# A gated linear attention and short convolution layer on one core: v and z_a with the rows of h as TensorE weights, block turns on VectorE, and two heads per attention step

## The chip, the core and the metric

The kernel runs on one core of a Trainium2 chip. The metric is device time in microseconds (us) for one execution; less is better. The engines are TensorE (PE, matmuls; PEld is its weight load), VectorE (DVE), ScalarE (ACT), GpSimd (POOL) and SyncE (SP, which issues the DMAs here). Each executes its own instructions strictly in order and waits on semaphores for the others.

## The reference

One layer (DEPTH = 1) on a sequence of 1024 rows of width 1024, all in float32:

```python
h = rms_norm(x, norm_mix_g)
q, k, v, z_a, gk_low, cb, cc, xc, z_c, g_a, g_c = split(h @ w_in)   # 512, 512, 1024, 1024, 16, 6 x 1024
gk = log_sigmoid(gk_low @ w_gk2 + b_gk) / 16
o = gla_chunked(q, k, v, gk)        # 4 heads, key width 128, value width 256, chunks of 64
o = rms_norm(o per head, gla_norm_g)
y_a = (o * silu(z_a)) @ w_branch_a
u = causal_dwconv3(cc * xc)
y_c = (cb * u * silu(z_c)) @ w_branch_c
merged = sigmoid(g_a + b_ga) * y_a + sigmoid(g_c + b_gc) * y_c
x = x + merged @ w_out
x = x + sigmoid(rms_norm(x, norm_ple_g) @ w_ple_gate) * (p @ w_ple_proj)
out = rms_norm(x, norm_final_g)
```

In `gla_chunked`, b is the running sum of gk within a chunk; q is scaled with exp(b), k with exp(-b) for the scores and with exp(b_last - b) for the state. The output is the masked scores times v plus scaled q times the state; the state decays by exp(b_last) per chunk and adds k^T v.

## The kernel before

**Numbers and products.** Float32 matmuls are done in three passes over a high and a low part (`split` at line 580 makes hi by a ScalarE copy and lo by a VectorE subtract; `mm3` at line 591 issues the three matmuls). The large products use a seven-product scheme of the Strassen kind on 2 x 2 blocks: h's seven combinations `hres[0..6]` (hi and lo, 512 x 512 each) stay in SBUF, and a `Cell` (line 704) computes 256 columns of a projection. It loads four weight blocks, `ring_steps` (line 663) makes the seven weight combinations, each split, and `product` runs twelve 512-column matmuls. In a cell the 128 columns of a weight combination are TensorE's stationary operand and the h rows (time) are the moving one, so the result has the projection's columns on partitions and time along the free axis. Each cell uses three PSUM banks: X, Y and V (tags m0 to m5, two sets in turn). Two more banks have the tag "o", two buffers, for everything else.

**Order.** Every instruction is first noted (`note`, line 260) and at the end put in order by a planner in the kernel (`put_in_order`, line 406), which has costs of its own and keeps the main matmuls in program order while it places the side ones among them; buffers of a tag are handed out in program order. `emit` (line 484) issues all of them, so the profile shows line 491 everywhere and one goes by names. Side work is given as generators: `weave` starts one, each `tick` (two per product) advances it, and `yield n` makes it wait for n ticks. DMAs are all issued on SyncE's queue.

**Stages.** (1) Start to 76 us: nine warm matmuls on zeros, p W_pe (`pe_blocks`, line 974), the norm of x in two halves (`scale_h`, line 943: squares, `ms` matmuls with ones, root on POOL and VectorE, `rt` transposes, scaling), two products of each of the eight gate cells (`two_products`, line 997; names ga0p to gc3p), and h's combinations. (2) 76 to 170 us: four v cells. `v_cons` (line 1037) copies each result block if needed, turns it with four 128 x 128 transposes on TensorE (matmuls against an identity, `pt_v`), splits it and stores it to DRAM (vd). `decays` (line 1059) runs woven beside them: for each half of the sequence `lowp` (16 matmuls), a copy `low`, four `zp` matmuls, one per head; for each pair of heads Abs, Exp and Ln on ScalarE, subtracts and scans on VectorE, and stores to DRAM (cd). It yields 2 after each zp and 4 after each pair. (3) 170 to 246 us: q and k cells, which read cd and store the scaled operands (qkd). (4) 246 to 322 us: four z_a cells; `za_cons` (line 1182) makes silu(z_a) times the norm's gain and stores it (szd). (5) 322 to 627 us: sixteen convolution cells, with w_out and w_ple_gate prepared beside them (wtd). (6) 627 to 780 us: gate cells, and woven among them attention (`attend`, line 1271), one head and 128 rows per step, with operands in four rotating buffers. A step transposes the keys on TensorE (X from ident and qkl), forms the scores, the state's growth and the output, and three steps later transposes the normed output (op from ident and og), multiplies it with silu(z_a) and stores it (od). (7) 780 to 935 us: y_c, then y_a with the merge. (8) From 935 us: the output projection, `flip` (line 1511), which transposes the new x on TensorE (`pt_g`) for the last gate, and that gate with the final norm.

Of the kernel before, what the change touches and what calls it, by code (L numbers as in the profile page):

```python
# [9 lines left out]
F32 = mybir.dt.float32  # L10
# [39 lines left out]
class View:  # L50


    def __init__(self, buf, rows, off, dims, dtype):
        self.buf, self.rows, self.off, self.dims, self.dtype = buf, rows, off, dims, dtype

# [75 lines left out]

    def place(self):
        real = self.buf.get()
        if self.dtype != self.buf.dtype:
# [368 lines left out]
def kernel(  # L503
# [4 lines left out]
    wb: bass.AP,  # L508
    wgl: bass.AP,
# [54 lines left out]
    qkd = [[dram(f"qkd{h}_{i}", NP, 5 * P) for i in range(2)] for h in range(H)]  # L564
    vd = [[dram(f"vd{h}_{i}", NP, 2, DV) for i in range(2)] for h in range(H)]
    szd = [[dram(f"szd{h}_{i}", NP, 2, P) for i in range(2)] for h in range(H)]
# [96 lines left out]
    def ring_steps(name, side, raw, fresh):  # L663
# [3 lines left out]
        def put(src):  # L667
            hi = bp.tile([P, 4, P], F32R, tag="whi", name=f"{name}hi", bufs=RING)
            lo = bp.tile([P, 4, P], F32R, tag="wlo", name=f"{name}lo", bufs=RING)
            split(hi, lo, src)  # L670
            return hi, lo
# [32 lines left out]
    class Cell:  # L704


        def __init__(self, name, side, src, res, cons, prods=ORDER, begin=None, s1=None, u2=None, s5=None, fresh=()):
# [5 lines left out]
            self.steps, self.fresh = ring_steps(name, side, self.raw, fresh), fresh  # L713
# [132 lines left out]


    def gate_cons(c, bias, dst):
        def cons(i, j, src):
            k = 2 * c + j  # L850
            t = ev(f"g{k}_{i}")
            act(t, src, AF.Sigmoid, bias=bias[:, k:k + 1])
            store(dst[k][i], t)
        return cons
# [12 lines left out]
    def merge_a(c, pool):  # L867
        def cons(i, j, src):
# [5 lines left out]
            tt(g, src, g, op=ALU.mult)  # L874
            if i == 0 and k >= 4:
                t = late[k - 4] = bp.tile([P, 512], F32, tag="raw", name=f"m{k}", bufs=8)
                tt(t, g, m, op=ALU.add)
                g = t
            else:
                tt(g, g, m, op=ALU.add)  # L880
            store(md[i][:, :, k // 4, :, k % 4, :], g.rearrange("p (a b t) -> p a b t", a=2, b=2))
# [5 lines left out]
    for n, name in enumerate([f"v{h}" for h in range(4)] + ["q0", "k0", "q1", "k1"] + [f"za{h}" for h in range(4)]  # L887
                             + [f"{m}{g}" for g in range(4) for m in ("cc", "xc", "zc", "cb")]
# [144 lines left out]

    with phase("v", [ph["prep0"]]) as qp:
        def v_cons(h):
            def cons(i, j, src):
                if j == 1:
                    t = src
                else:
                    t = ev(f"vt{h}_{i}_{j}")  # L1040
                    nc.scalar.copy(t, src)

                def flip():
                    pt = pso.tile([P, 4, P], F32, tag="o", name=f"pt_v{h}_{i}_{j}", bufs=2)
                    for s in range(4):
                        transpose(pt[:, s, :], t[:, s * P:(s + 1) * P])
                    hi = qp.tile([P, 4, P], F32R, tag="vhi", name=f"vhi{h}_{i}_{j}", bufs=2)
                    lo = qp.tile([P, 4, P], F32R, tag="vlo", name=f"vlo{h}_{i}_{j}", bufs=2)
                    split(hi, lo, pt)
                    js = slice(j * P, (j + 1) * P)  # L1050
                    store(vd[h][i][:, :, 0, js], f(hi))
                    store(vd[h][i][:, :, 1, js], f(lo))
                    return
                    yield

                weave(flip(), 2)
            return cons

        def decays():
# [14 lines left out]
            g2raw = qp.tile([P, 512], F32, name="g2raw")  # L1074
# [4 lines left out]
            yield 2  # L1079
            for half in range(2):  # L1080
# [14 lines left out]
                yield 2  # L1095
                for hp in range(2):
                    t1 = qp.tile([P, 2, HALF], F32, tag="t1", name=f"t1_{half}{hp}")
                    c = qp.tile([P, 2, HALF], F32, tag="c4", name=f"c4_{half}{hp}")
                    for i in range(2):
# [5 lines left out]
                        nc.vector.tensor_scalar(c[:, i, :], zp, bgk[:, h:h + 1], 0.0, op0=ALU.add, op1=ALU.min)  # L1105
                        yield 2
                    act(t1, t1, AF.Exp, scale=-1.0)
                    act(t1, t1, AF.Ln, bias=1.0)
                    for i in range(2):
                        tt(t1[:, i, :], t1[:, i, :], c[:, i, :], op=ALU.subtract)  # L1110
                        nc.vector.tensor_tensor_scan(c[:, i, :], smask, t1[:, i, :], 0.0, op0=ALU.mult, op1=ALU.add)
                        store(cd[2 * hp + i][half], c[:, i, :])
                    yield 4

        vs = [Cell(f"v{h}", "B", W[f"v{h}"], hres, v_cons(h)) for h in range(4)]
        vs[0].begin = lambda: weave(decays(), 1)
# [4 lines left out]
        run_groups(single(vs), single(qks[:2]))  # L1121
        finish_woven()

    with phase("qk", [ph["v"]]) as qp:
# [7 lines left out]
        def q_cons(hp):  # L1132


            def cons(i, j, src):
# [19 lines left out]
                store(qkd[h][i][:, :, 0:P], f(hi))  # L1155
                store(qkd[h][i][:, :, P:2 * P], f(lo))
                store(qkd[h][i][:, :, 2 * P:3 * P], Qf[:, :, P:2 * P])
            return cons

        def k_cons(hp):  # L1160

            def cons(i, j, src):
# [13 lines left out]
                store(qkd[h][i][:, :, 3 * P:5 * P], kk.rearrange("p n s t -> p n (s t)"))  # L1176
# [5 lines left out]
        def za_cons(h):  # L1182
            def cons(i, j, src):
                t = ev(f"sz{h}_{i}_{j}")
                act(t, src, AF.Sigmoid)
                stt(t, src, ggla[:, j:j + 1], t, op0=ALU.mult, op1=ALU.mult)
                store(szd[h][i][:, :, j, :], t.rearrange("p (n t) -> p n t", t=P))
            return cons

        zas = [Cell(f"za{h}", "B", W[f"za{h}"], hres, za_cons(h)) for h in range(4)]  # L1190
        run_groups(single(qks), single(zas[:2]))


    with phase("conv", [ph["qk"]]) as vp:
        def weights(vp):


            for w in range(2):
                for kt in range(4):
                    t = vp.tile([P, 4, 512], F32, tag="wt", name=f"wt{w}_{kt}", bufs=2)  # L1200
                    load(t, wb[w][:, :, kt, :].rearrange("n p c -> p n c"))
                    yield 14
                    b11, b12, b22, b21 = (t[:, n] for n in range(4))
                    if w:
                        for n, q in enumerate((b11, b12, b22, b21)):
                            k = kt + 4 * (n >= 2)
                            act(q, q, AF.Copy, scale=gple[:, k:k + 1])
                            if n != 1:
                                store(wtd[w][4 + (n + 1) // 2][:, kt, :], q)
                    tt(b11, b12, b11, op=ALU.subtract)  # L1210
                    yield 2
                    tt(b12, b22, b12, op=ALU.subtract)
                    yield 2
                    tt(b22, b22, b11, op=ALU.subtract)
                    yield 2
                    tt(b21, b21, b22, op=ALU.subtract)
                    for n, q in enumerate((b11, b22, b12, b21)):
                        store(wtd[w][n][:, kt, :], q)
                    yield 4

# [40 lines left out]

        gas, gcs = ([Cell(f"{m}{c}", "B", W[f"{m}{c}"], hres, gate_cons(c, bias, dst), prods=(1, 2, 4, 5, 6),
                          s1=s1d[n + c]) for c in range(4)]
                    for n, m, bias, dst in ((0, "ga", bga, gad), (4, "gc", bgc, gcd)))
        weave(weights(vp), 20)
        run_groups(single(zas + convs), pairs(gas[:2]))
        finish_woven()

    def attend(hp, ap, every):

        its = [(pr, 2 * hp + i) for pr in range(2 * NP) for i in range(2)]
        n, LAG = len(its), 3
        ins, szs, ogs, scores, S, Sp = {}, {}, {}, {}, {}, {}
        for i in range(2):
            h = 2 * hp + i
            S[h] = ap.tile([P, DV], F32, tag=f"S{i}", name=f"S{h}")  # L1280
            Sp[h] = (ap.tile([P, DV], F32R, tag=f"Sh{i}", name=f"Sh{h}"),
                     ap.tile([P, DV], F32R, tag=f"Sl{i}", name=f"Sl{h}"))

        def fetch(it):
            pr, h = its[it]
            nm = f"{h}_{pr}"
            qk = ap.tile([P, 5 * P], F32R, tag="qkl", name=f"qkl{nm}", bufs=4)
            v = ap.tile([P, 2, DV], F32R, tag="vl", name=f"vl{nm}", bufs=4)
            load(f(qk), qkd[h][pr // NP][:, pr % NP])
            load(f(v), vd[h][pr // NP][:, pr % NP])  # L1290
            ins[it] = qk, v

        def step_a(it, X):
            pr, h = its[it]
            qk = f(ins[it][0])
            mm(X[:, 0:P], qk[:, 3 * P:4 * P], qk[:, 2 * P:3 * P], start=True, stop=True)
            if pr < 2 * NP - 1:
# [401 lines left out]
```

## Time and profile before

| | |
|---|---|
| time, median of 3 runs | 1109.24 us (1108.81 to 1109.28) |
| span of the profiled execution | 1107.6 us (the page gives this span; what lies around it is not recorded) |
| TensorE busy | 1096.7 us (99%), 5113 records |
| VectorE busy | 857.5 us (77%), 1381 records |
| ScalarE busy | 592.5 us (53%), 1106 records |
| DMA moved | 235.81 MB, mean 213 GB/s |

The span is first to last instruction of one execution. Matmuls overlap in the pipeline, so the mean duration of one is longer than the distance between two starts. Rows of groups, the timeline and the chain of waits give, in this order, the engine, the operation, the tile written and those read (buffer numbers left out), the tile's shape and a count.

### The profile page before, as it was taken

What the parts mean: (1) busy time and instruction counts of PE and PEld (TensorE: products, weight loads), DVE (VectorE), ACT (ScalarE), POOL (GpSimd) and SP (SyncE); (2) the same over time, 40 slices, a digit from 0 to 9 for tenths busy, and PEclk for the clock granted to TensorE, in tenths of its full rate; (3) what the DMA queues carried; (4) which work ended last, traced back from release to release, by engine and by line L of the source; (5) the groups of instructions that cost most, each with busy time, mean ns of one, the idle gap of its engine ahead of it and who ended that gap; (6) DMA issues with size and microseconds to landing.
All of it is one profiled execution on the core that took longest, in us unless ns stands there. A gap on an engine that the chain in (4) does not pass through costs nothing.

```text
span 1107.6 us, 15420 instructions
## 1 busy us (share of the span) xinstructions
PE 1096.7 (99%) x5113; PEld 914.5 (83%) x5113; DVE 857.5 (77%) x1381; ACT 592.5 (53%) x1106; POOL 55.9 (5%) x121
## 2 busy tenths in 40 slices
PE   9999999999999999999999999999999999999996
PEld 7888888888888888888888888898888888888885
DVE  6997786997876856757648687876999879868666
ACT  6766765555464433333343376765836445457554
POOL 0000000000000000000000022230000000002012
PEclk9999999999999999999999999999999999999999
DMA  9943467988995131221312599998595888889753
GB/s 319 320 165 100 147 197 240 276 246 274 326 354 177 48 103 49 67 87 48 99 54 67 184 306 348 311 290 301 182 329 181 294 266 279 295 309 302 257 201 114
DMA packets 159040, 235.81 MB, mean 213 GB/s; under 512 B 12785, under 2 KB 74481, under 8 KB 155889
## 3 DMA queue, kind: packets, MB, share of 16 engines
q1 hardware_dynamic: 158960, 234.83, 64.0%
q8 instruction: 40, 0.66, 0.2%
q14 instruction: 40, 0.32, 0.1%
HBM read 154.04 MB, written 80.74 MB: 212 GB/s over the span
## 4 chain that ended last, share of the span: by engine, by line
PE 98%; DVE 1%; ACT 0%; DMA 0%; POOL 0%; issue 0%; POOLq 0%; DVEq 0%; ACTq 0%
PE op L491 3%; PE pe L491 2%; PE X L491 2%; PE ga3Y L491 1%; PE ga2Y L491 1%; PE ga1Y L491 1%; PE ga0Y L491 1%; PE out1Y L491 1%; PE gc1Y L491 1%; PE gc0Y L491 1%; PE out0Y L491 1%; PE out3Y L491 1%; PE v2Y L491 1%; PE v1Y L491 1%; PE out2Y L491 1%; PE v3Y L491 1%
## 5 line engine op out<-in xcount | busy, mean ns | idle before, releaser
L491 ACT ACTIVATE junk<-x 128x512 bf16<-128x512 f32 (+1 forms) x29 | 17.9, 616 | 13.6 <-DVE x L491 12.8
L491 POOL MEMSET t<- 128x2 f32 x8 | 0.8, 100 | 443.8 <-DVE u L491 270.9
L491 DVE TENSOR_TENSOR wt<-wt 128x512 f32<-128x512 f32 x32 | 21.6, 686 | 0.5 <-DMA zc0raw<-in_wc_dram 0.3
L491 POOL TENSOR_TENSOR or<-or,mhalf 128x1 f32<-128x1 f32 x32 | 20.4, 639 | 2.7
L491 DVE SCALAR_TENSOR_TENSOR u<-t,vec,u 128x1024 f32<-128x1024 f32 x16 | 20.4, 1277 | 0.0
L491 ACT ACTIVATE og<-op,or 128x256 f32<-128x256 f32 x32 | 15.1, 472 | 8.8 <-POOL or L491 6.5
L491 DVE COPY_PREDICATED aT<-trim,X 128x128 f32<-128x128 int32 x32 | 9.6, 301 | 12.8 <-PE X L491 12.4
L491 POOL TENSOR_SCALAR rg<-ms 128x1 f32<-128x1 f32 x8 | 4.8, 602 | 266.0 <-ACT junk L491 265.9
L491 ACT ACT_TABLE_LOAD x12 | 15.4, 1283 | 0.9 <-PEq L1688 0.7
L491 ACT CAST aTh<-aT 128x128 fp32r<-128x128 f32 x32 | 9.5, 298 | 11.2 <-DVE aT L491 9.7
L491 PE MATMUL op<-vl,aTh 128*128 128x256 f32 x64 | 15.0, 314 | 0.0
L491 POOL TENSOR_SCALAR or<-oms 128x1 f32<-128x1 f32 x32 | 8.8, 275 | 119.0 <-ACT junk L491 119.0
L491 PE MATMUL op<-Sh,qkl 128*128 128x256 f32 x56 | 14.6, 283 | 0.0
L491 DVE TENSOR_TENSOR oT<-op,szl 128x256 f32<-128x256 f32 x32 | 13.4, 420 | 1.0 <-DMA od<-oT 0.6
L491 ACT ACTIVATE junk<-op 128x256 bf16<-128x256 f32 x32 | 12.3, 385 | 2.0 <-PE op L491 1.6
L491 PE MATMUL pe<-wpehi,pThi 128*128 128x512 f32 x32 | 13.1, 409 | 0.0
L491 DVE TENSOR_TENSOR Sl<-S,Sh 128x256 fp32r<-128x256 f32 x28 | 11.8, 420 | 1.4 <-ACT Sh L491 1.3
L491 DVE TENSOR_TENSOR vlo<-pt_v,vhi 128x512 fp32r<-128x512 f32 x16 | 10.6, 681 | 2.8 <-ACT vhi L491 2.8
L491 PE MATMUL pe<-wpelo,pThi 128*128 128x512 f32 x32 | 12.8, 400 | 0.0
L491 PE MATMUL pe<-wpehi,pTlo 128*128 128x512 f32 x32 | 12.7, 398 | 0.0
L491 PEld LDWEIGHTS X<-vl,keh 128*128 128x128 f32 x56 | 10.5, 188 | 2.3
L491 PE MATMUL X<-qkl 128*128 128x128 f32 x64 | 12.3, 273 | 0.0
(3245 smaller groups left out, 4183.6 us busy)
## 6 DMA issues: line engine op xcount, KB each, us to landing
wtd<-wt SPq DMA_DIRECT2D x44, 256.0 KB, 4.0
qkl<-qkd SPq DMA_DIRECT2D x32, 320.0 KB, 5.1
wt<-in_wb_dram SPq DMA_DIRECT2D x8, 1024.0 KB, 7.0
vl<-vd SPq DMA_DIRECT2D x32, 256.0 KB, 5.1
wgq<-wtd SPq DMA_DIRECT2D x7, 1024.0 KB, 8.3
uq<-ud SPq DMA_DIRECT2D x5, 1024.0 KB, 5.5
oq<-od SPq DMA_DIRECT2D x5, 1024.0 KB, 6.7
hq<-in_xT_dram SPq DMA_DIRECT2D x8, 512.0 KB, 6.9
```

What stands on the lines that cost most here:

```text
L491: o.call(*[place(a) for a in o.args], **{k: place(a) for k, a in o.kw.items()})
```

## The change

- **v and z_a** are no longer cells. A new function `wide` computes all 1024 columns of each with h's rows as the stationary operand and the weights as the moving one (512 columns), so the results have time on partitions. Four row blocks are in work at once: eight PSUM banks, the fourth of each set of four with tag "o". The seven products run in the order 0, 3, 1, 2, 5, 4, 6. z_a follows v directly; q and k come after it. The blocks need no transpose: v is split and stored, z_a becomes z times sigmoid(z).
- **decays** yields 1 everywhere; its c tile is now one buffer per head with two buffers in all.
- **k**'s state operand is turned in blocks of 32 x 32 on VectorE and put in place by the DMA's addresses (ked). So are attention's output and the operand of the last gate; the columns of the a-gates, w_ple_gate and its norm gain are permuted to match.
- **attention** takes two heads per step, reads its operands through two rotating buffers in the slots of hres 0 and 3, multiplies the output with silu(z_a) ahead of the turn, and yields 3 per step. The norm's gain is applied later, as twenty ScalarE scalings of 128 x 512 when y_a's operands are read.

The diff, cut to its core:

```diff
+    def put_blocks(dst, start, dims, src):
+        store(dst.spread(start, dims), src)
...
+    def wide(name, w, pool, cons):
+        raw, ring, keep = {}, {}, {}
...
+        def product(k, acc, start):
+            rhi, rlo = hres[k]
+            for kt in range(4):
+                whi, wlo = ring.pop((k, kt))
+                for b in range(4):
+                    bs = slice(b * P, b * P + P)
+                    nc.side = False
+                    mm3(acc[b], rhi[:, kt, bs], rlo[:, kt, bs], whi, wlo, start and kt == 0, kt == 3)
+                    nc.side = True
+                    if b % 2:
+                        tick()
...
+        first, second = ("m0", "m1", "m2", "o"), ("m3", "m4", "m5", "o")
+        near = [(bp, "u2"), (bp, "u2"), (bp, "s5"), (bp, "s5")]
+        prep(0)
+        X = four("X", first)
+        prep(3)
+        product(0, X, True)
+        x0 = copies("x", X, near)
+        prep(1)
+        product(3, X, False)
+        for b in range(4):
+            cons(0, 0, b, X[b])
+        prep(2)
+        V = four("V", second)
+        product(1, V, True)
+        Y = four("Y", first)
+        for b in range(4):
+            nc.scalar.copy(Y[b], x0[b])
+        c22 = copies("s", V, [(bp, "s5"), (bp, "s5"), (pool, "ws"), (pool, "ws")])
...
-                def flip():
-                    pt = pso.tile([P, 4, P], F32, tag="o", name=f"pt_v{h}_{i}_{j}", bufs=2)
-                    for s in range(4):
-                        transpose(pt[:, s, :], t[:, s * P:(s + 1) * P])
...
+        def v_cons(i, j, b, src):
+            hi = qp.tile([P, 512], F32R, tag="vhi", name=f"vhi{i}_{j}_{b}", bufs=2)
+            lo = qp.tile([P, 512], F32R, tag="vlo", name=f"vlo{i}_{j}_{b}", bufs=2)
+            split(hi, lo, src)
+            for n, t in enumerate((hi, lo)):
+                store(vd[j][i][:, b, :, n, :], f(t).rearrange("p (h d) -> p h d", h=2))
...
-                    c = qp.tile([P, 2, HALF], F32, tag="c4", name=f"c4_{half}{hp}")
+                    c = [qp.tile([P, HALF], F32, tag="c4", name=f"c4_{half}{hp}{i}", bufs=2) for i in range(2)]
...
-                        yield 2
+                        yield 1
...
-                    yield 4
+                    yield 1
...
-        vs[0].begin = lambda: weave(decays(), 1)
+        weave(decays(), 1)
+        wide("v", [wv[0, n] for n in range(4)], qp, v_cons)
+        finish_woven()
+        wide("za", [wv[1, n] for n in range(4)], qp, z_cons)
...
+                nc.vector.transpose(turned.rearrange("p b n c -> p n b c"),
+                                    kf[:, :, P:2 * P].rearrange("p n (b c) -> p n b c", c=32))
+                for g in range(4):
+                    put_blocks(ked[hp][i][:, j, g * P:g * P + P], j * 512 + g * P, [(32 * 1024, 4), (1, P)],
+                               turned[32 * g:32 * g + 32].rearrange("p b n c -> p b (n c)"))
...
+        vb, qb = slot(0, "h", f"v{hp}", (2, 1024)), slot(0, "l", f"qk{hp}", (2, 1024))
...
+            for h in range(2):
+                stt(sz[:, h], op[:, h], r[:, h:h + 1], sz[:, h], op0=ALU.mult, op1=ALU.mult)
...
+            nc.vector.transpose(turns[i][:, :, m, :], sz.rearrange("p h (b c) -> p (h b) c", c=32))
...
+            if s and s + 1 < n:
+                fetch(s + 1)
+            yield 3
...
+            if gain is not None:
+                for kt in range(4):
+                    act(t[:, kt, :], t[:, kt, :], AF.Copy, scale=gain[:, kt % 2:kt % 2 + 1])
...
-                pt = pso.tile([P, 4, P], F32, tag="o", name=f"pt_g{p}_{i}_{j}", bufs=2)
-                for k in range(4):
-                    transpose(pt[:, k, :], xt[i][j][:, k * P:(k + 1) * P])
-                g = lp.tile([P, 4, P], F32, tag="gr", name=f"gr{p}_{i}_{j}", bufs=3)
-                nc.scalar.copy(g, pt)
-                store(gd[p][j][:, i], g)
+                g = lp.tile([P, 16, 32], F32, tag="gr", name=f"gr{p}_{i}_{j}", bufs=3)
+                nc.vector.transpose(g, xt[i][j].rearrange("p (b c) -> p b c", c=32))
+                for a in range(4):
+                    put_blocks(gd[p][j][:, i, a, :], i * 512 + a * P, [(32 * 1024, 4), (1, P)],
+                               g[32 * a:32 * a + 32].rearrange("p (b k) c -> p b (k c)", k=4))
```

More of the change, by code (lines that the diff above doesn't have):

```diff
@@ L130, in blocks, with spread @@
         return sorted({b for s in starts for b in range(s // GRAIN, (s + step * (n - 1)) // GRAIN + 1)})
+    def spread(self, start, dims):
+        v = View(self.buf, self.rows, self.off, self.dims, self.dtype)
+        v.apart = start, dims
+        return v
     def place(self):
         real = self.buf.get()
+        if self.apart:
+            start, dims = self.apart
+            return bass.AP(tensor=real.tensor, offset=real.offset + start,
+                           ap=[[self.buf.size, 32]] + [[s, n] for s, n in dims])
         if self.dtype != self.buf.dtype:
@@ L508 @@
     wb: bass.AP,
+    wv: bass.AP,
     wgl: bass.AP,
@@ L1032, with need, put, prep @@
     nc.vector.tensor_scalar(ggla, ggla, float(P) ** -0.5, None, op0=ALU.mult)
-    with phase("v", [ph["prep0"]]) as qp:
[L1035 to L1041, printed above, removed]
-                def flip():
-                    pt = pso.tile([P, 4, P], F32, tag="o", name=f"pt_v{h}_{i}_{j}", bufs=2)
-                    for s in range(4):
-                        transpose(pt[:, s, :], t[:, s * P:(s + 1) * P])
[L1047 to L1057, printed above, removed]
+    def wide(name, w, pool, cons):
+        raw, ring, keep = {}, {}, {}
+        def need(n, kt):
+            raw[n, kt] = bp.tile([P, 512], F32, tag="raw", name=f"{name}raw{n}_{kt}", bufs=8)
+            load(raw[n, kt], w[n][:, kt, :])
+        def put(k, kt, src):
+            hi = bp.tile([P, 512], F32R, tag="whi", name=f"{name}{k}hi{kt}", bufs=RING)
+            lo = bp.tile([P, 512], F32R, tag="wlo", name=f"{name}{k}lo{kt}", bufs=RING)
+            split(hi, lo, src)
+            ring[k, kt] = hi, lo
+        B11, B12, B22, B21 = range(4)
+        def prep(k):
+            for kt in range(4):
+                if k in (0, 3, 6):
+                    need(B11 if k == 0 else B21, kt)
+                elif k in (1, 2):
+                    need(B12 if k == 1 else B22, kt)
+                at = lambda n: raw[n, kt]
+                if k == 1:
+                    keep[kt] = bp.tile([P, 512], F32, tag="T", name=f"{name}T{kt}", bufs=4)
+                    tt(keep[kt], at(B12), at(B11), op=ALU.subtract)
+                elif k == 2:
+                    tt(keep[kt], at(B22), keep[kt], op=ALU.subtract)
+                elif k == 4:
+                    tt(at(B12), at(B22), at(B12), op=ALU.subtract)
+                elif k == 6:
+                    tt(keep[kt], at(B21), keep[kt], op=ALU.subtract)
+                put(k, kt, keep[kt] if k in (1, 2, 6) else at({0: B11, 3: B21, 4: B12, 5: B22}[k]))
+        def product(k, acc, start):
[9 more added lines that the diff above has]
+                        tick()
+        def four(what, tags):
+            return [psm.tile([P, 512], F32, tag=t, name=f"{name}{what}{b}", bufs=2 if t == "o" else 1) for b, t in enumerate(tags)]
+        def copies(what, acc, tags):
+            out = []
+            for b in range(4):
+                where, tag = tags[b]
+                t = where.tile([P, 512], F32, tag=tag, name=f"{name}{what}{b}", bufs=2)
+                nc.scalar.copy(t, acc[b])
+                out.append(t)
+            return out
+        first, second = ("m0", "m1", "m2", "o"), ("m3", "m4", "m5", "o")
[13 more added lines that the diff above has]
+        Y = four("Y", first)
+        for b in range(4):
+            nc.scalar.copy(Y[b], x0[b])
+        c22 = copies("s", V, [(bp, "s5"), (bp, "s5"), (pool, "ws"), (pool, "ws")])
+        prep(5)
+        product(2, Y, False)
+        c12 = copies("u", Y, [(bp, "u2"), (bp, "u2"), (pool, "wu"), (pool, "wu")])
+        prep(4)
+        product(5, V, False)
+        for b in range(4):
+            tt(c12[b], V[b], c12[b], op=ALU.add)
+            cons(0, 1, b, c12[b])
+        prep(6)
+        product(4, Y, False)
+        for b in range(4):
+            tt(c22[b], Y[b], c22[b], op=ALU.add)
+            cons(1, 1, b, c22[b])
+        product(6, Y, False)
+        for b in range(4):
+            cons(1, 0, b, Y[b])
@@ L1073, in decays @@
                 split(glw[:, 8:12, i, 0:16], glw[:, 8:12, i, 16:32], gdif)
-            g2raw = qp.tile([P, 512], F32, name="g2raw")
+            g2raw = qp.tile([P, 512], F32, tag="low", name="g2raw")
             load(g2raw, wgk2)
@@ L1180 @@
             qks[2 * hp].cons, qks[2 * hp + 1].cons = q_cons(hp), k_cons(hp)
[L1182 to L1219, printed above, removed]
+        vp = phase("conv", [ph["qk"]])
         convs = []
@@ L1260, with weights @@
                 convs.append(Cell(f"{m}{g}", "B", W[f"{m}{g}"], hres, cons, begin=cc_begin if m == "cc" else None))
+        run_groups(single(qks), single(convs[:2]))
+    with vp:
+        def weights(vp):
+            for w in range(2):
+                for kt in range(4):
+                    t = vp.tile([P, 4, 512], F32, tag="wt", name=f"wt{w}_{kt}", bufs=2)
+                    load(t, wb[w][:, :, kt, :].rearrange("n p c -> p n c"))
+                    yield 14
+                    b11, b12, b22, b21 = (t[:, n] for n in range(4))
+                    if w:
+                        for n, q in enumerate((b11, b12, b22, b21)):
+                            k = kt + 4 * (n >= 2)
+                            act(q, q, AF.Copy, scale=gple[:, k:k + 1])
+                            if n != 1:
+                                store(wtd[w][4 + (n + 1) // 2][:, kt, :], q)
+                    tt(b11, b12, b11, op=ALU.subtract)
+                    yield 2
+                    tt(b12, b22, b12, op=ALU.subtract)
+                    yield 2
+                    tt(b22, b22, b11, op=ALU.subtract)
+                    yield 2
+                    tt(b21, b21, b22, op=ALU.subtract)
+                    for n, q in enumerate((b11, b22, b12, b21)):
+                        store(wtd[w][n][:, kt, :], q)
+                    yield 4
         gas, gcs = ([Cell(f"{m}{c}", "B", W[f"{m}{c}"], hres, gate_cons(c, bias, dst), prods=(1, 2, 4, 5, 6),
@@ L1397 @@
     with phase("att", [ph["conv"]]) as ap:
-        aTf = [ap.tile([P, P], F32, name=f"aT{i}") for i in range(2)]
+        aTf = [ap.tile([P, 2, P], F32, name=f"aT{i}") for i in range(2)]
         for a in aTf:
@@ L1645, in _lay_out @@
     col = lambda m, n: m[:, n * 256:n * 256 + 256]
-    cells = [col(v, h) for h in range(4)]
+    cells = []
     for hp in range(2):
         cells += [col(q, hp), col(k, hp)]
-    cells += [col(za, h) for h in range(4)]
     for g in range(4):
```

270 lines of the change are left out of this document (132 added, 138 removed).

## The prediction

> **What bounds the kernel now.** I read the page first: busy times, granted clock and the chain that ended last.
>
> ```profile
> span 1107.6 us, 15420 instructions
> PE 1096.7 (99%) x5113; PEld 914.5 (83%) x5113; DVE 857.5 (77%) x1381; ACT 592.5 (53%) x1106; POOL 55.9 (5%) x121
> PEclk9999999999999999999999999999999999999999
> PE 98%; DVE 1%; ACT 0%; DMA 0%; POOL 0%; issue 0%; POOLq 0%; DVEq 0%; ACTq 0%
> ```
>
> TensorE (PE) is busy 1096.7 of 1107.6 us, at full clock in every slice, and holds 98% of the chain. A share over the whole span can hide a stage with slack, so I next took the windows by stage (columns: stretch, its length, then busy time and instructions of PE, PEld, VectorE (DVE), ScalarE (ACT) and POOL, the clock, the DMA share and GB/s).
>
> ```profile
> 30.00:76.00 46.00, 46.00 (x215) 38.35 (x213) 43.51 (x57) 33.47 (x48) 1.02 (x1) 1.00 0.75 260
> 76.00:170.00 94.00, 93.99 (x442) 76.70 (x441) 76.67 (x119) 63.01 (x101) 0.64 (x2) 1.00 0.51 154
> 170.00:246.00 76.00, 76.00 (x339) 62.93 (x338) 63.36 (x127) 42.23 (x88) 0.00 (x0) 1.00 0.84 254
> 627.00:780.00 153.00, 153.00 (x877) 134.02 (x875) 114.60 (x266) 99.69 (x269) 29.24 (x64) 1.00 0.91 301
> 780.00:860.00 80.00, 80.00 (x354) 66.27 (x353) 78.17 (x103) 47.02 (x68) 0.00 (x0) 1.00 0.71 238
> ```
>
> These are the end of the gate preparation, the v cells with the decays, the q and k cells, attention, and the stage after it. PE has no hole in any of them. So PE work that goes is gained in full, and every wait the new order puts before a matmul is lost in full. VectorE is the next bound: 43.51 of 46, and 78.17 of 80 after attention.
>
> **What goes.** The transposes on PE, 220 in all, are these groups (last columns: busy us, mean ns, idle before).
>
> ```profile
> L491 PE MATMUL op<-ident,og 128*128 128x128 f32 x64 | 12.3, 273 | 0.0
> L491 PE MATMUL X<-ident,qkl 128*128 128x128 f32 x28 | 7.6, 273 | 0.0
> L491 PE MATMUL pt_g<-ident,x 128*128 128x128 f32 x48 | 7.4, 272 | 0.0
> L491 PE MATMUL pt_v<-ident,vt 128*128 128x128 f32 x32 | 5.0, 273 | 0.0
> L491 PE MATMUL pt_g<-ident,x2r 128*128 128x128 f32 x16 | 2.4, 272 | 0.0
> ```
>
> The other 32 for v carry names of partial sums (v0s and the like). The 273 ns is no price, because matmuls overlap; what counts is the distance from start to start, in the timeline:
>
> ```profile
> 102.22 0.28 PE L491 MATMUL pt_v<-ident,vt 128*128 128x128 f32 x1
> 102.33 0.64 PE L491 MATMUL pt_v<-ident,v0s 128*128 128x128 f32 x4
> 102.81 0.49 PE L491 MATMUL pt_v<-ident,vt 128*128 128x128 f32 x3
> 103.06 0.47 PE L491 MATMUL v1V<-h1hi,v1hi 128*128 128x512 f32 x1
> 103.37 0.39 PE L491 MATMUL v1V<-h1lo,v1hi 128*128 128x512 f32 x1
> ```
>
> Eight transposes take 103.06 - 102.22 = 0.84 us (0.105 each), or 0.115 each if the late start of the second v1V matmul is theirs. So 220 x 0.11 = **24.2 us less PE work** (23.1 to 25.3). All other matmuls stay in number and size, v and za included; only weights and moving operand change places. Their price, with a cold one beside it, is in the chain of waits:
>
> ```profile
> 1.44 4.21 PE warm L491 x9
> 76.39 2.72 PE v0X L491 x12
> 92.49 3.73 PE lowp L491 x16
> ```
>
> A 512-column matmul takes 2.72/12 = 0.227 us; the first nine of the kernel, just after idleness, 4.21/9 = 0.468.
>
> **What is added, hidden or not.** VectorE gets 40 block turns of 512 elements, for which no row stands. The nearest are 0.69 (128x512 subtract, below) and 1.22 (scan, below); I take the first, since a turn has no carry from element to element: 28 us, of which merging two heads into one instruction in attention gives part back. VectorE has 857.5 of 1107.6, so this is hidden if it falls evenly: 8 turns in the q and k stage (5.5 to 9.8 us against 12.6 idle there), 16 in attention (38 idle), 16 at the output. ScalarE loses the transposes' evictions and gets 20 scalings of attention's output (about 0.6 each by the copy row below, 12 us in a stage where it is half idle). SyncE's queue gets 28 more DMAs, many with runs of 512 bytes. I put 1.0 us for what of all this is not covered (0 to 10).
>
> **Start, 0 to 76 us.** The planner reorders it, as the instruction order shows. Before:
>
> ```profile
> 16.99 1.23 DVE L491 TENSOR_TENSOR sq<-sq 128x1024 f32<-128x1024 f32 x1 [0.37 <-ACT sq L491]
> 19.40 1.68 PE ms L491 x16
> 21.08 2.44 PE pe L491 x10
> 71.93 1.21 DVE L491 TENSOR_TENSOR hq<-hq,hq 128x1024 f32<-128x1024 f32 x1
> 73.06 1.21 DVE L491 TENSOR_TENSOR h4lo<-hq,h4hi 128x1024 fp32r<-128x1024 f32 x1
> ```
>
> The sum of squares is ready at 18.22, and the ms matmuls come after 57 pe matmuls. Now they come after 48: 9 x 0.24 = 2.2 us earlier, at 17.2, so PE waits 1.0. The root behind ms (POOL, then VectorE) was covered by ten matmuls (2.44); three are left (0.7), so PE waits up to 1.7, which I take whole: the rows show that ten matmuls cover it, not with how much to spare. Later, four more splits of h (pitch 73.06 - 71.93 = 1.13, 4.5 us) stand ahead of the split that the second gate product needs, in a stretch where VectorE is 95% busy; earlier v splits no longer stand there, which gives back most: 1.8 (0 to 4.5). **Start: +4.5** (1.0 to 7.2).
>
> **The v stage.** Four row blocks now share two sets of PSUM banks. The fourth bank of each set carries the tag "o" with two buffers, handed out in program order: X3, lowp, four zp, lowp, four zp, V3, Y3. The decays yield every tick, so all of them are noted within the first two products, and PE executes in order. What was beside PE work before now stands before matmuls. Durations, from the timeline of before and the tile views of cd (the last line but one) and vd (the last):
>
> ```profile
> 131.47 0.58 ACT L491 COPY v2s<-v2V 128x512 f32<-128x512 f32 x1
> 131.95 0.69 ACT L491 ACTIVATE t<-zp,vec 128x512 f32<-128x512 f32 x1
> 132.65 1.28 ACT L491 ACT_TABLE_LOAD   x1
> 132.67 0.75 DVE L491 TENSOR_SCALAR c<-zp,vec 128x512 f32<-128x512 f32 x1 [0.18 <-ACT t L491]
> 133.95 1.06 ACT L491 ACTIVATE t<-t 128x1024 f32<-128x1024 f32 x1
> 136.02 1.28 ACT L491 ACT_TABLE_LOAD   x1
> 137.31 1.06 ACT L491 ACTIVATE t<-t 128x1024 f32<-128x1024 f32 x1
> 138.41 0.69 DVE L491 TENSOR_TENSOR t<-t,c 128x512 f32<-128x512 f32 x1 [2.17 <-ACT t L491]
> 140.22 1.22 DVE L491 TENSOR_TENSOR_SCAN c<-smask,t 128x512 f32<-128x512 f32 x1
> DMA to landing us min/median/max: 2.1/3.7/5.1
> DMA to landing us min/median/max: 2.6/4.2/6.8
> ```
>
> Table load and function are 2.34 us together. Step by step, by the order of instructions:
> - Product 3 may write X1 to X3 only after ScalarE has copied them out; the copies stand between two table pairs: 4 x 0.58 + 2 x 2.34 = 7.0 us against 19 matmuls (4.3). Part of an Abs (0.69) lies ahead of it: **3.05** (2.7 to 3.4).
> - Second half's zp0 waits for low's copy, which stands behind Abs, both table pairs and two copies: 3 x 0.58 + 2 x 2.34 + two or three VectorE pieces (1.4 to 2.1) = 7.8 to 8.5, against lowp (3.73) and 8 matmuls (1.82): **2.45**.
> - zp1 needs X3's bank, freed by the fourth vlo, behind two scans and two splits on VectorE: 2 x 1.22 + 3 x 0.69 = 4.5, less zp0's own 0.2 and 0.08 for each piece, the difference of pitch and duration above: **3.9** (3.5 to 4.3); zp2 waits 0.5 for zp0's eviction.
> - V3 needs the bank of zp2. Its eviction (c of the second pair) needs c's buffer, which the first pair's scan result leaves only once stored to cd. From zp1: Abs 0.69, two table pairs 4.68, two subtracts 1.3, scan 1.2, landing 2.1 to 5.1, eviction 0.75 = 10.7 to 13.7, less 0.7 of matmuls: 10.0 to 13.0. I take **10.5**, nearer the short end, since the DMA share is only 0.51 here. Behind V3 stand all remaining matmuls of v.
>
> Sum 20.4 (18.9 to 24.2). **At za's first product**, X1 and X2 wait for the last v splits: vhi and vlo have two buffers each, and a third split waits until the first is stored. A cast (as the 0.58 copy), landing 2.6 to 4.2, cast and split of the third block (1.3) and a weight's split between (0.69) make 5.1 to 6.7, against 15 matmuls (3.4): 1.7 to 3.3. Two blocks wait in turn, so I go near the long end: **3.2**.
>
> **Cold clock.** No row of before shows PE after an idle of 10 us except the kernel's start: nine matmuls at 0.468 instead of 0.227 lose 2.2 us. I take that once, after V3's wait (0 to 4.4).
>
> The Trainium skill, "TensorE: Matmul & The Clock Gate", section "Why this matters for your kernels", warns of PE idle gaps above about 3 us, after which the clock falls to half. By it the clock would fall once or more here; the start row agrees with it, while no gap of before can test it.
>
> **Sum**, against the profiled span: 1107.6 - 24.2 + 4.5 + 20.4 + 3.2 + 2.2 + 1.0 = 1114.7. The time median (1109.24) lies 1.6 above that span, which I keep: **1116.3 us**, 0.6% slower. With all ends one way: 1107.6 - 25.3 + 1.0 + 18.9 + 1.7 = 1103.9 (1105.5 as time), and the other way 1107.6 - 23.1 + 7.2 + 24.2 + 3.3 + 4.4 + 10 = 1133.6 (1135.2).
>
> **Rivals.**
> A, faster: V3's wait does not bite, because the second pair's eviction comes soon enough: if ScalarE and VectorE reach the first pair's chain while PE still waits elsewhere, V3 finds its bank at about 2 us instead of 10.5, and the clock doesn't fall: 1116.3 - 8.5 - 2.2 = 1105.6, and 1102 with the start's 4.5 at its short end of 1.0. It decides once 7.1 of the 31.3 us that I add are gone: under 24.2 in all the change gains. For it: VectorE has 17 and ScalarE 31 idle us in the v window. Against: each link names the one before it. 0.24.
> B: attention is now fetched into two buffers, not four. A step of two heads takes 153/16 less its transposes, about 8.9 us, and that is what a load has.
>
> ```profile
> qkl<-qkd SPq DMA_DIRECT2D x32, 320.0 KB, 5.1
> wgq<-wtd SPq DMA_DIRECT2D x7, 1024.0 KB, 8.3
> ```
>
> Now 512 KB, so 5.1 to 8.3; with a DMA share of 0.91 and an issue kept back 1.5 us behind other waits of SyncE's queue (my assumption), 14 steps late by 0.9 make +12.6: 1129. For: the share. Against: loads were no wait before. 0.10.
> C: VectorE becomes the bound where turns fall on full stretches (q and k, and after attention): the 9.8 us of turns come out whole: 1116.3 + 9.8 - 1.0 = 1125. Against: PE was at 100% beside a VectorE at 98%. 0.09.
> D: the clock falls at each of four waits of 3 us or more, 2.2 each, three more than counted: 1116.3 + 6.6 = 1123. The Trainium skill's section named above is the rule for this; only the kernel's start bears it out. 0.13.
> E: the waits and the transposes cancel (stalls at their short ends, clock kept, start as worked): 1105.5 + 3.5 = 1109. 0.08.
> The forecast itself: 0.36.
>
> **Numbers.** About 0.2% (2.2 us) is what a measurement of this kernel can tell from no change. Slower by more: 0.36 + 0.10 + 0.09 + 0.13 = 0.68; within: 0.08; faster: 0.24. The range goes from 1101 (just under A's short end) to 1130 (past B): outside lie some 0.1 below, where two of the v waits would be missing, and 0.08 above.
>
> **What would show it.** Right: in the profile after, PE busy about 24 us less; holes in PE of 3, 2.5, 4 and 10 us between about 85 and 115 us, each ended by ScalarE or VectorE of the decays or by low, a hole of 3 us before za; matmuls after the longest at twice the distance; attention some 10 us shorter. Wrong: no hole before V3 (A), PE waits for qk loads (B) or for VectorE at q, k and after attention (C), a granted clock under 1.00 in several places (D).

## The result, and the profile after

The changed kernel takes **1155.12 us** (1154.31 to 1155.79) against 1109.26 us for the kernel before: ratio 1.0412, 95% interval 1.0397 to 1.0427, so 46 us slower. The direction was forecast, the size was not: it lies far above the range (1101 to 1130). The profiled execution spans 1153.1 us, 45.5 more than before. First the page of the kernel after:

```profile
span 1153.1 us, 14771 instructions
PE 1087.9 (94%) x4893; PEld 896.8 (78%) x4893; DVE 873.8 (76%) x1359; ACT 586.4 (51%) x1037; POOL 48.0 (4%) x89
PEclk9999699999999999999999999999699999999999
PE 79%; DMA 8%; DVE 5%; ACT 3%; SPq 2%; issue 1%; POOL 0%; POOLq 0%; DVEq 0%; ACTq 0%
```

PE's share of the chain fell from 98% to 79%, and the granted clock has two dips where before it had none. VectorE, which got the turns, is at 76% of the span: it did not become the bound. The waits of PE, one row for each thing waited for (us in total, times, longest), with the eight longest:

```profile
PE yc0X L502 <- ACT u0hi L502: 16.1, 1, 16.1
PE vV L502 <- DVE c L502: 8.5, 1, 8.5
PE zaX L502 <- DVE vlo L502: 3.7, 2, 2.0
PE gt0Y L502 <- DVE gt0s L502: 3.7, 1, 3.7
PE zp L502 <- DVE vlo L502: 3.4, 1, 3.4
PE zp L502 <- DVE low L502: 2.8, 1, 2.8
PE vX L502 <- ACT vx L502: 2.7, 2, 1.9
PE out2Y L502 <- ACT gt0hi L502: 2.3, 1, 2.3
```

The v and z_a rows are those that the prediction worked out; those of the start are shorter ones (1.4 before pe, 1.4 before gc1p, 0.8 before ms). The longest of all, u0hi before y_c, is not in it. The eight come to 43.2 us. The transposes that went were worth some 24 us (worked out below), so about 70 us were lost in all; the rest are shorter waits and matmuls at half clock.

By stage, from the first matmul of each to the first of the next: the start took 82.34 us (76.22 before); v and z_a together 192.9 (168.7); q and k 76.3 (77.1); the convolution 305.7 (304.6); the gates with attention 163.6 (158.7); y_c 86.0 (76.2); y_a 76.2 (76.2); the output 79.8 (83.1); the last gate to the end 90.4 (86.7). So 6 us are lost at the start, 24 in v and z_a, 15 from attention to the end of y_c, and nothing at the output and last gate together, although the transposes, some 24 us, went from three of these stages.

**The v stage.** The chain of waits up to V3's first matmul (start, length, what; the ACT rows without a name are table loads):

```profile
126.28 0.69 ACT t L502
126.98 1.28 ACT L502
128.28 1.06 ACT t L502
129.35 1.28 ACT L502
130.65 1.06 ACT t L502
...
131.74 1.29 DVE t L502 x2
133.03 1.15 DVE c L502
134.19 1.98 DMA cd<-c
...
136.27 0.76 DVE c L502
...
137.07 3.35 PE vV L502 x7
```

Each link is one of the sum for V3: Abs, two table loads with Exp and Ln, subtracts, a scan, the store to cd, and the eviction that frees the bank. From 126.28 to 137.07 it is 10.8 us, at the short end of the 10.7 to 13.7 worked out.

**From attention to y_c.** In the timeline, attention's steps begin at their first kv matmul. Two of them, then the end of attention and the start of y_c:

```profile
787.44 0.40 PE L502 MATMUL kv<-v,keh 128*128 128x256 f32 x2
...
797.08 0.40 PE L502 MATMUL kv<-v,keh 128*128 128x256 f32 x2
...
804.30 0.39 PE L502 MATMUL gc3Y<-h6hi,gc3lo 128*128 128x512 f32 x1
...
807.66 0.71 DVE L502 STREAM_TRANSPOSE oT<-szl 128x512 f32<-128x512 f32 x1
808.40 3.23 SPq L502 DMA_DIRECT2D od<-oT  x4
811.73 2.63 SPq L502 DMA_DIRECT2D uq<-ud  x3
...
819.68 1.99 ACT L502 CAST u0hi<-uq 128x1024 fp32r<-128x1024 f32 x2 [13.61 <-DMA uq<-ud]
...
820.78 0.79 PE L502 MATMUL yc0X<-u0hi,yc0hi 128*128 128x512 f32 x1 [16.08 <-ACT u0hi L502]
```

These two steps are 9.6 us apart. So are most others, or 11.0; the exceptions stand where a pair of heads begins (4.6, 17.0 and 6.2). Attention's last matmuls end near 803.8, 0.9 us ahead of the last of the gate cells; only then are its outputs turned and stored, and behind these stores on SyncE's queue the loads of y_c's operand uq are issued, the first of which lands 7.9 us later. VectorE had nothing to do in this hole either: it was idle for 12.4 us until u0hi came. In the kernel before, the loads of uq were issued 25 us ahead of y_c's start:

```profile
760.49 1.37 SPq L491 DMA_DIRECT2D uq<-ud  x3
...
785.44 0.39 PE L491 MATMUL yc0X<-u0hi,yc0hi 128*128 128x512 f32 x1
```

### The profile page after: what moved, and what is told of

Its sections match the earlier page's. It is cut to its first block, busy times and chain, and to the rows that moved or that the text cites. A ratio compares the mean times of both kernels' runs of the same rounds, so it can differ in the third digit from the quotient of the medians.

```text
span 1153.1 us, 14771 instructions
## 1 busy us (share of the span) xinstructions
PE 1087.9 (94%) x4893; PEld 896.8 (78%) x4893; DVE 873.8 (76%) x1359; ACT 586.4 (51%) x1037; POOL 48.0 (4%) x89
## 4 chain that ended last, share of the span: by engine, by line
PE 79%; DMA 8%; DVE 5%; ACT 3%; SPq 2%; issue 1%; POOL 0%; POOLq 0%; DVEq 0%; ACTq 0%
PE vY L502 3%; PE zaY L502 2%; PE zaX L502 2%; PE vV L502 2%; PE zaV L502 2%; PE op L502 2%; SPq L502 2%; PE vX L502 1%; PE pe L502 1%; DMA wtd<-wt 1%; PE kv L502 1%; DMA gt1raw<-gd 1%; DMA x<-in_x_dram 1%; DMA wgq<-wtd 1%; PE ga3Y L502 1%
## 5 line engine op out<-in xcount | busy, mean ns | idle before, releaser
L502 PE MATMUL yc0X<-u0hi,yc0hi 128*128 128x512 f32 x4 | 2.7, 669 | 16.1 <-ACT u0hi L502 16.1
L502 DVE TENSOR_TENSOR t<-t,c 128x512 f32<-128x512 f32 x8 | 5.3, 689 | 16.0 <-ACT t L502 15.9
L502 ACT CAST S<-S 128x512 fp32r<-128x512 f32 x14 | 8.6, 618 | 13.7 <-PE op L502 13.7
L502 PE MATMUL vV<-v1hi,h1hi 128*128 128x512 f32 x16 | 7.4, 460 | 8.5 <-DVE c L502 8.5
L502 DVE SCALAR_TENSOR_TENSOR szl<-op,or,szl 128x256 f32<-128x256 f32 x32 | 14.0, 476 | 0.9 <-POOL or L502 0.9
L502 PE MATMUL op<-S,qk 128*128 128x256 f32 x84 | 14.5, 281 | 0.0
L502 DVE TENSOR_TENSOR x<-x,pe 128x512 f32<-128x512 f32 (+1 forms) x17 | 11.1, 655 | 2.9 <-DMA x<-x2d 2.7
L502 ACT ACTIVATE oq<-oq,vec 128x512 f32<-128x512 f32 x20 | 13.0, 712 | 0.0
L502 PE MATMUL op<-v,aTh 128*128 128x256 f32 x64 | 12.6, 280 | 0.0
L502 DVE SCALAR_TENSOR_TENSOR S<-S,dds,kv 128x256 f32<-128x256 f32 x24 | 10.4, 475 | 2.3 <-PE kv L502 2.3
L502 PEld LDWEIGHTS op<-S,qk 128*128 128x128 f32 x84 | 11.9, 188 | 0.0
```

The costliest lines, as they stand in the source:

```text
L502: o.call(*[place(a) for a in o.args], **{k: place(a) for k, a in o.kw.items()})
```

## The experiments

Theory 1: the loss has two causes apart from each other. One is the decays beside a wide product that holds the same two PSUM banks (v, and through the planner's order the start). The other is attention's two operand buffers: a step can't begin until qk has landed in the buffer that the step before last has left, so attention ends late, and y_c's operand with it. This works through the planner's order: the loads of after landed 0.8 to 21 us ahead of the score matmuls that read them, so PE waited for none of them. The distances of the steps are the same to 0.01 us in after, deep, v_cells and flip_pe, since the planner had put that many gate matmuls between them. The rivals are written into each expectation.

**Attention's load in halves (qk_halves).** The score half of qk is used one step earlier than the q half, so it can be fetched earlier into the same memory.

```diff
-            load(f(qk), qkd[hp][s // NP][:, s % NP])
+            for c in (2 * P, 0):
+                load(f(qk[:, :, c:c + 2 * P]), qkd[hp][s // NP][:, s % NP, :, c:c + 2 * P])
```

> Attention's qk load is split in two (score half, then q half), so that the score half of step s+1 can start one step earlier; nothing else changes. Theory 1 (attention's steps are spaced by the landing of qk, 6.4 us, in two buffers; attention so ends late, and y_c's first operand u0, which takes a slot that attention holds, comes late): steps go from about 10 us apart to about 7, attention ends some 40 us earlier, the 16.1 us wait for u0hi and most of the 10 us lost in the y_c stage go: about 1129 us (1125 to 1134). Rival (u0 is late because VectorE or the DMA engines are full there): under 8 us gained, 1147 or more.

Measured 1131.81 us (ratio to before 1.0200, 1.0176 to 1.0225): 23 us gained. The timeline of qk_halves, two steps, and its first waits:

```profile
728.10 0.40 PE L502 MATMUL kv<-v,keh 128*128 128x256 f32 x2
...
733.66 0.40 PE L502 MATMUL kv<-v,keh 128*128 128x256 f32 x2
```

```profile
PE vV L502 <- DVE c L502: 8.5, 1, 8.5
PE gt0Y L502 <- DVE gt0s L502: 5.6, 1, 5.6
```

Steps come 5.6 us apart here, 6.5 at most within a pair of heads, u0hi is no longer waited for at all, and y_c takes 76.16 us as before. The window of y_c in qk_halves (length, then busy time of PE, PEld, VectorE, ScalarE and POOL, clock, DMA share, GB/s), and the time from issue to landing of the qk loads in after and in qk_halves, in this order:

```profile
809.00:885.00 76.00, 76.00 (x337) 62.96 (x336) 71.63 (x94) 49.67 (x76) 0.00 (x0) 1.00 0.66 232
DMA to landing us min/median/max: 4.1/6.4/7.7
DMA to landing us min/median/max: 2.7/6.1/7.6
```

VectorE is busy for 71.6 of these 76 us, and half a qk still takes 6.1 us to land: neither a full VectorE nor the transfer itself was the trouble, but when the load could start. Theory 1 holds for this half, in the form that the order of instructions counts with the load; that the planner's own cost of a load sets that order is argued from its code.

**Tiles of their own for the decays' second pair (deep).** The wide v stays; only the buffers of the decays change, so that the second pair's evictions don't wait for the first pair's scans and stores.

```diff
-                    t1 = qp.tile([P, 2, HALF], F32, tag="t1", name=f"t1_{half}{hp}")
-                    c = [qp.tile([P, HALF], F32, tag="c4", name=f"c4_{half}{hp}{i}", bufs=2) for i in range(2)]
+                    if hp:
+                        t1 = [qp.tile([P, HALF], F32, tag="wu", name=f"t1_{half}{hp}{i}", bufs=2) for i in range(2)]
+                    else:
+                        t1 = qp.tile([P, 2, HALF], F32, tag="t1", name=f"t1_{half}{hp}")
+                        t1 = [t1[:, i, :] for i in range(2)]
+                    c = [qp.tile([P, HALF], F32, tag="ws" if hp else "c4", name=f"c4_{half}{hp}{i}", bufs=2) for i in range(2)]
...
-                    act(t1, t1, AF.Exp, scale=-1.0)
-                    act(t1, t1, AF.Ln, bias=1.0)
+                    for i in range(2):
+                        act(t1[i], t1[i], AF.Exp, scale=-1.0)
+                    for i in range(2):
+                        act(t1[i], t1[i], AF.Ln, bias=1.0)
...
```

> The decays' second pair of heads gets tiles of its own (of tags that are free until later), so it doesn't wait for the first pair's scans and stores; its Exp and Ln are issued per head. Theory 1 (V3 waits for a bank through the first pair's chain to the store; the planner hurries h's parts forward at the start because that chain is due): V3's 8.5 us wait falls to 2 to 4, the half clock after it goes (2.2), the start gets the order of before (about 5 back): about 1140 us (1135 to 1146). Rival (ScalarE's table loads or the fourth vlo hold the banks in any case): the wait moves to the next bank, under 4 us gained, 1151 or more.

Measured 1136.60 us (1.0238, 1.0218 to 1.0258): 18.5 gained. The first waits of deep:

```profile
PE yc0X L502 <- ACT u0hi L502: 16.1, 1, 16.1
PE gt0Y L502 <- DVE gt0s L502: 4.6, 1, 4.6
PE zaX L502 <- DVE vlo L502: 3.7, 2, 2.0
PE zp L502 <- ACT t L502: 3.6, 2, 1.9
PE zp L502 <- DVE c L502: 2.1, 1, 2.1
```

V3's wait is gone whole; 5.7 us before zp remain. v's first matmul comes at 75.83 us (82.34 after), with the ms matmuls behind 57 pe matmuls again: the late start was a consequence of the decays' chain, without any edit to the start. That the planner hurried h's parts because the chain was due early is argued from its code; that the start goes with the chain is shown, here and in the next run.

**v in cells again (v_cells).** v's 64 transposes on TensorE and the decays' yields of 2 and 4 come back; z_a stays wide.

```diff
...
-                        yield 1
+                        yield 2
...
-                    yield 1
-
-        weave(decays(), 1)
-        wide("v", [wv[0, n] for n in range(4)], qp, v_cons)
+                    yield 4
+
+        vs = [Cell(f"v{h}", "B", W[f"v{h}"], hres, v_cons(h)) for h in range(4)]
+        vs[0].begin = lambda: weave(decays(), 1)
+        run_groups(single(vs))
         finish_woven()
...
```

> v is made in cells again, turned by 64 TensorE transposes, with the decays' old yields; z_a stays wide, all else stays. Theory 1 (the v stage's waits come from decays beside a wide product that holds the same two banks): the waits in v go (some 20 us), with the half clock (2.2 or more) and the start's loss (about 5), and 64 x 0.11 = 7 us of transposes come back: about 1134 us (1129 to 1140); the waits in z_a's first product stay. Rival (the wide form is itself slower, z_a included): gain under 10 us, 1145 or more.

Measured 1125.58 us (1.0141, 1.0121 to 1.0160): 29.5 gained, more than the expected range. The first waits of v_cells:

```profile
PE yc0X L502 <- ACT u0hi L502: 16.1, 1, 16.1
PE gt0Y L502 <- DVE gt0s L502: 2.6, 1, 2.6
```

PE waits for nothing from 30 us to the end of z_a: the waits before z_a's first product, which I expected to stay, went too. v takes 93.6 us (92.6 before) and the wide z_a 76.9, 0.7 more than its cells took. So the wide form costs next to nothing by itself; what cost was a wide v beside the decays, and v's last split in two buffers ahead of z_a. This run changes the cells, the transposes and the decays' yields at once: what the yields alone would do in a wide v was not tried. That the chain through the shared banks is at work is shown by deep, which leaves the wide form and the yields as they are.

**The last gate's turn on TensorE (flip_pe).**

```diff
-                g = lp.tile([P, 16, 32], F32, tag="gr", name=f"gr{p}_{i}_{j}", bufs=3)
-                nc.vector.transpose(g, xt[i][j].rearrange("p (b c) -> p b c", c=32))
...
+                pt = pso.tile([P, 4, P], F32, tag="o", name=f"pt_g{p}_{i}_{j}", bufs=2)
+                for k in range(4):
+                    transpose(pt[:, k, :], xt[i][j][:, k * P:(k + 1) * P])
...
```

> The turn for the last gate goes back to 64 TensorE transposes and 16 stores. Theory 1 (the waits at the output, 0.8, 2.3 and 3.7 us, come from the turned stores and the loads behind them): 7.0 us of transposes come back and about as much waiting goes: 1155 us (1153 to 1157). Rival (those waits come from VectorE's adds and stay): 1162 us.

Measured 1156.09 us (1.0419, 1.0403 to 1.0434): 1 us slower than the change, within the expected. The waits of gt0Y, out2Y and out3V (3.7, 2.3 and 0.8 us) are gone from the list and 7 us of transposes are back. Turned on VectorE, this step is worth nothing here.

**Both fixes (both_fixes, both_fixes_flip_pe, wide_deep_halves).** These join the edits above and have no new one.

> The two edits that gave most, together: v in cells with the decays' old yields, and attention's qk load in halves; z_a wide, two heads per step and all block turns on VectorE stay but v's. Theory 1 (the two losses are apart in time and cause): 1125.6 less the 25 us of u0's wait and the ragged y_c stage: about 1100 us (1096 to 1104), under the kernel before by some 0.8%. Rival (PE merely meets VectorE or the DMA engines elsewhere once these waits are gone): no faster than before, 1109 or more.

Measured 1099.28 us; ratio to before 0.9907, 0.9892 to 0.9923. This beats the kernel before, by 0.9%, and the change by 56 us. Its page, and all the waits of its PE:

```profile
span 1097.4 us, 14939 instructions
PE 1081.3 (99%) x4957; PEld 898.8 (82%) x4957; DVE 871.2 (79%) x1359; ACT 585.4 (53%) x1041; POOL 47.8 (4%) x89
```

```profile
PE gt0Y L502 <- DVE gt0s L502: 3.7, 1, 3.7
PE warm L502 <- DVE zero L502: 1.4, 1, 1.4
PE out2Y L502 <- DVE x L502: 1.2, 1, 1.2
```

PE is the bound again.

> As both_fixes, and the turn for the last gate back on TensorE (64 transposes). Theory 1 (turned stores and transposes cost the same there): within 2.5 us of both_fixes. Rival (the waits for the last gate were a remnant of the late start of that stage and go anyway): 7 us slower than both_fixes.

Measured 1099.81 us (0.9916, 0.9902 to 0.9929): the same as both_fixes, with no wait but that for the first zeros. Its span, 1098.3 us, is 9.3 below before's with 92 transposes fewer (28 of k, 64 of attention's output): 0.101 us for each, net of the waits and slow matmuls in which the two differ.

> v and z_a wide, no transpose on TensorE: the decays' second pair with tiles of its own and attention's qk load in halves. Theory 1: 1136.6 less 25: about 1111 us (1107 to 1116), level with the kernel before or a little slower, because waits of about 10 us stay around the wide products (zp, z_a's first product) with a half clock behind them. Rival (these waits go too once attention's loads are out of the planner's due times): 1103 or less.

Measured 1109.68 us (1.0004, 0.9995 to 1.0012): level with the kernel before, as expected. With no transpose on TensorE at all, the waits around the wide products (3.6 and 2.1 before zp, 3.7 in z_a), the 5.4 before gt0Y and the half clock behind them take back the whole gain.

## Why the prediction was right or wrong

**Right: the bound and the method.** PE had no slack, so each wait was lost in full. The four waits of the v stage were forecast at 3.05, 2.45, 3.9 with 0.5, and 10.5, in sum 20.4; measured were 2.7, 2.8, 3.4 with 0.9, and 8.5, in sum 18.3, at the places and with the engines named. z_a's was 3.2 and is 3.7; the start 4.5 and is 6.1, of which 3.9 are waits (0.8 before ms, 1.7 between ms and rt, 1.4 before gc1p) near the places named. The gate cells ended 147.5 us after their first matmul, 11.2 sooner than before: attention's stage itself was shorter by what was forecast. The turn was taken at 0.69 us, and the groups of the kernel after have 0.71:

```profile
L502 DVE STREAM_TRANSPOSE oT<-szl 128x512 f32<-128x512 f32 x16 | 11.3, 706 | 0.3
```

The price of the transposes holds: in before the median distance from the start of a matmul with ident to the next start is 0.108 us, 23.8 us for 220. The 0.101 above is a net figure.

**Wrong: the term "1.0 us for what of all this is not covered (0 to 10)".** It covered attention's two buffers and everything behind them. Measured in its place: 16.1 us before y_c, 7.4 more inside y_c (9.8 less 12 matmuls at half clock), and 6.8 at the output and the last gate. Rival B named the right cause, the two buffers, with a chance of 0.10, but put the price in the wrong place. I let PE stand still 0.9 us in each of 14 steps. It did not: the planner lets gate matmuls go between the steps, so PE was busy all through attention, and the steps stood about 10 us apart, where qk_halves does with 5.6. The debt fell due at the end, where y_c's operand needs attention's memory: by the code uq lies in the memory of attention's phase and u0hi in the slot of hres 0, and the trace shows the load of uq as what came last. I had noted that attention takes the slots of hres 0 and 3 and did not ask who needs them next, nor at what time attention's last step would stand in the order of instructions, which was there to be read: in before it ended some 35 us before the gate cells did, in after with them. The term was put at 1.0 with no row for it.

**Wrong: the clock.** I counted one fall (2.2 us). At half clock the distance of 512-column matmuls is 0.427; after the first 10 us, 36 matmuls of the kernel after have about that distance, 36 x 0.2 = 7.2 us. They stand at the start, behind V3's wait, behind z_a's two waits and behind u0hi's. So rival D held in size (its four falls are 8.8 us), but not in its places: z_a's waits were under 2 us each, and the one of 3.7 us before gt0Y had no fall behind it. A sign that I had named also failed: PE's busy time fell by 8.8 us, not by 24, in part because a slow matmul counts as busy for longer (0.63 us in the last rows below, against 0.40). This is a miss apart from attention's: qk_halves, where attention's part is gone, still takes 15.5 us more than the forecast and lies just above its range. Its trace has 52 matmuls at that distance (10.4 us), its v begins 10.5 us later than in before, and 5.6 us are waited before gt0Y.

**The sum with measured terms**, against the span: 1107.6 - 23.8 + 6.1 + 18.3 + 3.7 + 6.6 of clock (7.2 less what lies within the start's 6.1) + 16.1 + 7.4 + 6.8 = 1148.8, of 1153.1. Of the 4.3 us that are missing, 3.1 lie in how a wait is counted: as idle time the waits of v, z_a, u0hi, the output and the last gate come to 44.9 us, but from start to start, less 0.227 for a matmul, to 48.1. The rest I did not place.

**What the two causes cost** is confirmed by their removal: 23 and 29.5 us one by one, together 55.8 (1155.12 to 1099.28), which is more than their sum by 3.0; half-clock stretches, which differ from run to run, are large enough for that; that they are the reason is not shown.

## What to carry to other kernels

When side work is spread between the main matmuls of a busy engine, a slower buffer doesn't show as idle time there: it shows where that work has to be finished, so read in the order of instructions when its last step comes, and who takes its memory next. Work that shares a rotating set of buffers with a long-lived tile has to finish before that tile is handed out, and its whole latency then stands in the path. A turn on another engine saves the transposes (0.11 us each here) only where nobody waits for the result.

## What the runs showed of the hardware

In these traces the half clock needed no single long gap. Before z_a's third block PE stood still twice, 1.96 and 1.75 us with three matmuls between, in the timeline of after:

```profile
194.53 0.50 PE L502 MATMUL zaX<-za0hi,h0hi 128*128 128x512 f32 x1 [1.96 <-DVE vlo L502]
194.87 0.40 PE L502 MATMUL zaX<-za0lo,h0hi 128*128 128x512 f32 x1
195.11 0.39 PE L502 MATMUL zaX<-za0hi,h0lo 128*128 128x512 f32 x1
197.25 0.79 PE L502 MATMUL zaX<-za0hi,h0hi 128*128 128x512 f32 x1 [1.75 <-DVE vlo L502]
197.84 0.63 PE L502 MATMUL zaX<-za0lo,h0hi 128*128 128x512 f32 x1
198.27 0.63 PE L502 MATMUL zaX<-za0hi,h0lo 128*128 128x512 f32 x1
```

After the first gap the distance is 0.23 again, after the second 0.43, for a dozen matmuls. The Trainium skill, "TensorE: Matmul & The Clock Gate", section "Why this matters for your kernels", sets the danger at gaps above about 3 us; here two shorter ones close together did it, while the 3.7 us gap before gt0Y in the same execution did not; in both_fixes a gap of 3.7 us there was followed by 11 matmuls at 0.43. It also varies from one execution to another: with the same instruction order up to there, the ga0p products began at 36.62 us in after and at 41.02 in qk_halves, where the granted clock was 0.63 from 20 to 30 us and 0.74 from 30 to 42 (0.83 and 1.00 in after). So short gaps can cost more than their length. They may also be what scatters the times: qk_halves ran from 1129.34 to 1134.6 us, and the execution with this slow start is the one of 1134.6.
